# A gated trunk of three token mixers on one core: a score product on all 128 rows, and tiles laid at multiples of 128 bytes

## Chip, core and metric

The kernel runs on one core of a Trainium2 chip. The metric is the device time of one execution in microseconds; of several executions the median counts.

## What is computed

One layer over 1024 positions of 1024 channels, in float32. The input is normalised, one wide projection makes all operands, three branches mix the positions, each branch is gated and projected, and the merged sum goes through an output projection. The part that matters here is branch C, causal attention with 8 heads of 64 channels and a forgetting gate:

```python
h = rmsnorm(x, norm_g)
p = h @ w_in                       # gate_pre, a_in, a_z, b_uv, b_z, q, k, v, c_z, f_pre
q, k = rmsnorm(q, qn_g), rmsnorm(k, kn_g)          # per head of 64
c = cumsum(log_sigmoid(f_pre + b_f))               # per head
s = (q @ k.T) / 8 + c[query] - c[key]              # causal mask
o = softmax(s) @ v
y_c = (o * silu(c_z)) @ w_c
# y_a: GLU -> causal depthwise convolution (31 taps) -> layernorm -> silu, gated
# y_b: u * (tril(W_s) v + b) in chunks of 128 positions, gated
x = x + (g_a * y_a + g_b * y_b + g_c * y_c) @ w_out
```

## The kernel before

Float32 products are made of three products of a rounded type of the same four bytes: each operand is the sum of its rounding (hi) and the rest (lo), and hi x hi, hi x lo and lo x hi are added in one accumulator. So every weight tile comes as `raw` by DMA, is rounded by ScalarE (`w_hi`, L136), and GpSimd subtracts (`w_lo`, L137). `gemm_T` (L149) multiplies 128 output channels by 512 positions, with the normalised input `h_hi`, `h_lo` or a branch's operand as the moving tile.

The order of the stages is: the input's norm and transposes with the products for v (L267, L268); the projections of the first q and k; the gating unit's v and the mixing of positions (L404, L417); the attention; branch C's gate and projection together with branch A's GLU and its convolution on VectorE (31 taps, L646 and L649); branch B's second half; the norm of branch A; the merges; the output projection (L772). The instructions of all engines are put in order ahead of time by a planner with costs of its own, from the dependences between tiles and the priorities that the code gives. A tile that takes the place of an older one waits until the older one has no more readers. In the attention the heads have priority, and gates (`gate_pre`), the next heads' q and k and the gating unit's u (`u_slab`) are set between their products.

For a pair of heads, `stacks` builds 128-row operands. For head e of the pair its own 64 rows are `own`, the others `oth`. `ka` holds k hi on both halves; `qa` holds q hi on `own` and q lo on `oth`. So one product of 128 rows (L491) gives q hi x k hi + q lo x k hi. The third part, q hi x k lo, is a second product into the same accumulator with the 64 rows of `own` alone (L492), from a tile `kl` that the two heads of a pair share, each with its half. `head` goes through the query blocks from the last to the first, in up to two spans of keys; behind each span come the maximum (L494, VectorE), the exponential (L497, ScalarE), the scaling by the sum (L510, GpSimd), the transposes (L520), their rounding (L525, L526) and the product with v (L531).

The constants' pool comes first in the memory of a partition. Its square tiles have 512 bytes each, `eps` has 4, `vec` 168 and `cwT` 496; the pools for weights, h and what follows lie behind it, others are stacked from the other end of the memory. The moving tiles and the weights are multiples of 512 bytes, but for those of the products for v and the gating unit's v: `wv`, `wv_hi` and `wv_lo` have 520 columns, 2080 bytes.

Of the kernel before, what the change touches and what calls it, by code (L numbers as in the profile page):

```python
# [8 lines left out]
F32 = mybir.dt.float32  # L9
F32R = mybir.dt.float32r  # L10
# [5 lines left out]
P = 128  # L16
EPS = 1e-6
BIG = 3.0e38
NEG = -1.0e30
PRIO = 4000  # L20
# [7 lines left out]
def trunk_kernel(ctx, tc, x, norm_g, w_in, b_gate, conv_w, conv_b, conv_norm_g, conv_norm_b,  # L28
                 w_a, gmlp_norm_g, w_s, b_s, w_b, q_norm_g, k_norm_g, b_f, w_c, w_out, out):
    """float32 products are taken as three float32r passes: an operand is the exact sum of its  # L30
    rounding to 12 significant bits (hi) and the rest (lo), which has 12 bits as well, and
    hi*hi + hi*lo + lo*hi leaves out lo*lo alone, under float32's own rounding."""
# [28 lines left out]
    def f32(ap):  # L61
        return ap.bitcast(F32)

    # ---------------------------------------------------------------- pools
    # left: const, wpool, h, mix, then what a phase needs; right: v and o, later the merged sum
# [3 lines left out]

    const = ctx.enter_context(tc.tile_pool(name="const", bufs=1))  # L70
    wpool = ctx.enter_context(tc.tile_pool(name="wpool", bufs=3))
# [13 lines left out]
    # ---------------------------------------------------------------- constants  # L85
# [14 lines left out]
    eps = const.tile([P, 1], F32, name="eps")  # L100
    nc.vector.memset(eps, EPS)
    NVEC = 42
    vec = const.tile([P, NVEC], F32, name="vec")
    cwT = const.tile([P, JA, KW], F32, name="cwT")

    def newton(out_, ms, y0, y2, a, eng=None):
        """out_ = y0 brought nearer to (ms + EPS) ** -0.5."""
        if eng is None:
            nc.scalar.activation(y2, y0, AF.Square)
        else:  # L110
            eng.tensor_tensor(y2, y0, y0, op=ALU.mult)
        nc.vector.scalar_tensor_tensor(a, ms, EPS, y2, op0=ALU.add, op1=ALU.mult)
        nc.vector.tensor_scalar(a, a, -0.5, 1.5, op0=ALU.mult, op1=ALU.add)
        if out_ is not None:
            nc.vector.tensor_tensor(out_, y0, a, op=ALU.mult)

    def rsqrt(out_, ms, y0, y2, a):
        """out_ = (ms + EPS) ** -0.5: from the tables, then a Newton step."""
        nc.scalar.activation(y0, ms, AF.Ln, bias=eps)
        nc.scalar.activation(y0, y0, AF.Exp, scale=-0.5)  # L120
        newton(out_, ms, y0, y2, a)

    # ---------------------------------------------------------------- slabs of weights
    KH = 4

    def slab(src, kchunks, c0):
        """128 columns of a [kchunks * 128, n] matrix as hi and lo, K on partitions, KH chunks a tile."""
        out_ = []
        v = src.rearrange("(kc p) n -> p kc n", p=P)
        with tc.high_priority(offset=2 * PRIO):  # L130
            for k0 in range(0, kchunks, KH):
                raw = wpool.tile([P, KH, P], F32, name="raw")
                nc.sync.dma_start(out=raw, in_=v[:, k0:k0 + KH, c0:c0 + P])
                hi = wpool.tile([P, KH, P], F32R, name="w_hi")
                lo = wpool.tile([P, KH, P], F32R, name="w_lo")
                nc.scalar.copy(hi, raw)  # L136
                nc.gpsimd.tensor_tensor(lo, raw, f32(hi), op=ALU.subtract)  # L137
                out_.append((hi, lo))
        return out_

    def gemm_T(w, act, evac):
        """evac(half, psum, tokens): 128 output channels on partitions, 512 tokens."""
        for hf in range(NHALF):
            ps = mm.tile([P, HALF], F32, name="ps", tag="mm")
            ts = slice(hf * HALF, (hf + 1) * HALF)
            for kc in range(len(w) * KH):
                wk, k = w[kc // KH], kc % KH
                for n, (a, b) in enumerate(((0, 0), (0, 1), (1, 0))):
                    nc.tensor.matmul(ps, lhsT=wk[a][:, k, :], rhs=act[b][:, kc, ts],  # L149
                                     start=kc == 0 and n == 0, stop=kc == len(w) * KH - 1 and n == 2)  # L150
            evac(hf, ps, ts)

    # ---------------------------------------------------------------- q and k, normalised
# [25 lines left out]
    # ---------------------------------------------------------------- x -> h^T, v and f  # L179
    wnat = w2.rearrange("(kc p) n -> p kc n", p=P)  # L180
    cT_d = dram.tile([NH, S], F32, name="cT_d")
    # gates taken as far as their products between the attention's heads
    # (branch, chunk): the gates in the order in which they are wanted
# [3 lines left out]
    with ExitStack() as ph:  # L187
# [3 lines left out]
        NV = DC + NH  # L191
        N1 = DC // 2
        gb = p0.tile([P, D], F32, name="gb")
        bfb = p0.tile([P, NH], F32, name="bfb")
# [6 lines left out]
        class Weights:  # L201
            """hi and lo of columns c0.. of w_in (with those of f), a tile for every 128 rows, by way of mixT."""

            def __init__(self, c0, n, f0=None):
# [3 lines left out]
                last = p0x.tile([P, NV], F32, name="wv", bufs=1)  # L208
# [8 lines left out]
            def split(self, kc, eng):  # L217
                hi = p0x.tile([P, NV], F32R, name="wv_hi", bufs=KC)[:, 0:self.n]
                lo = p0x.tile([P, NV], F32R, name="wv_lo", bufs=KC)[:, 0:self.n]
                nc.scalar.copy(hi, self.raw[kc])  # L220
                eng.tensor_tensor(lo, self.raw[kc], f32(hi), op=ALU.subtract)
                self.hi.append(hi)
                self.lo.append(lo)
# [4 lines left out]
        def norm(i, r, pieces):  # L228
            """h of tile i in the place of x, in four steps"""
# [13 lines left out]
        def trans(i):  # L243
            """h^T of tile i, in two steps"""
# [10 lines left out]
        def prod(i, w, lag=0):  # L255
            """products of tile i with v and f, a step for every 128 rows of the weights, lo of them lag steps later"""
# [27 lines left out]
        with tc.high_priority(offset=8 * PRIO), tc.manual_schedule(engines=START):  # L284
            # norm, transposes and products of the tiles take turns, the first two of them in the order in which the
            # weights come in; the tensor engine's clock rises with work, which may as well be done before there is any
# [42 lines left out]
        # per-channel vectors, channel on partition  # L329
# [20 lines left out]
        # log sigmoid(z) = min(z, 0) - log1p(e), e = exp(-|z|);  # L350
        # log1p(e) = 2 atanh(s) = 2 s (1 + s^2/3 + s^4/5 + ...), s = e / (2 + e) <= 1/3
# [23 lines left out]
        # the scores stand at 8 times their value until the exponential  # L375
# [5 lines left out]
        # branch B's first half: v of the gating unit, its norm and the mixing of positions  # L381
        bsb = p0.tile([P, NG, P], F32, name="bsb")
        wsT = p0.tile([P, NG, 2, P], F32R, name="wsT")
# [44 lines left out]
    # ---------------------------------------------------------------- forgetting attention  # L428
    with ExitStack() as ph:
# [10 lines left out]
        for t in phis + plos:  # L440
            nc.gpsimd.memset(f32(t[:, 0, :]), 0.0)
        turn = [0, 0]

        def stacks(p, qn, kn):
            kl = stk.tile([P, S], F32R, name="kl", bufs=1)
            res = []
            for e in range(2):
                own = slice(e * HD, (e + 1) * HD)
                oth = slice((1 - e) * HD, (2 - e) * HD)
                ka = stk.tile([P, S], F32R, name="ka")  # L450
# [20 lines left out]
        def head(h, st, vc, oT):  # L471
# [3 lines left out]
            # from the last query block to the first: a block's own keys, once masked, are not asked for again  # L475
            for g in reversed(range(NT // 2)):
                pr = [None, None]
                for t in (2 * g + 1, 2 * g):
# [4 lines left out]
                    # a second span of 256 keys at least, which a float32r product's full rate asks for  # L483
# [3 lines left out]
                    for ci, (c0, n) in enumerate(spans):  # L487
# [4 lines left out]
                        nc.tensor.matmul(s[:, 0:w], lhsT=qa[own, qs], rhs=kl[own, cs], start=False, stop=True)  # L492
                        # the query's own cumulative gate is the same for all its keys, and goes with the maximum
# [7 lines left out]
                    else:  # L501
                        # two spans of keys, each by its own maximum, brought to the greater one
# [11 lines left out]
                for k2 in range(g + 1):  # L514
                    # the last pair of key blocks has nothing for the first query block in its second half
# [61 lines left out]
    # ---------------------------------------------------------------- branch C operand, branch A's input  # L577
# [3 lines left out]
    def gated(dst, src, w, tmp):  # L581
        """dst hi and lo = src * silu(h w); src takes the product."""
# [19 lines left out]
    # ---------------------------------------------------------------- merge  # L602
# [3 lines left out]
    def gate(bi, d, dst):  # L606
        """dst(half): where a half of the gate goes."""
# [22 lines left out]
    # ---------------------------------------------------------------- branch A: GLU and convolution; merge of C  # L630
# [30 lines left out]
    # ---------------------------------------------------------------- branch B: second half  # L661
# [7 lines left out]
    # ---------------------------------------------------------------- branch A: norm; merge of B  # L669
# [38 lines left out]
    # ---------------------------------------------------------------- branch A: gate and merge  # L708
# [47 lines left out]
    # ---------------------------------------------------------------- output projection  # L756
    ox_ctx, ox = pool("ox", bufs=3)
    for nh in range(D // HALF):
        ns = slice(nh * HALF, (nh + 1) * HALF)
        hi, lo = wos[nh]  # L760
        for i in range(NT):
# [3 lines left out]
            # the last tile in two pieces, for less to be left after the last product  # L765
# [46 lines left out]
```

## Time and profile before

| | |
|---|---|
| three runs | 1154.55, 1164.84, 1168.1 us, median 1164.84 |
| profiled execution | span 1162.8 us from the first to the last instruction; what lies around it isn't shown |
| mean granted TensorE clock | 0.984 |
| TensorE busy | 1116.7 us (96%), 5248 matmuls |
| VectorE, ScalarE, GpSimd busy | 606.8 us (52%), 462.0 us (40%), 501.5 us (43%) |
| products of 512 columns | L149: 3264, L404: 192, L772: 360 |
| score products | L491: 96, L492: 96 |

A span is counted from the first instruction to the last. Busy times overlap between engines, and matmuls overlap each other, so that a sum of their durations is more than the time they take.

### The profile page before, as it was taken

What the parts mean: (1) busy time and instruction counts of PE and PEld (TensorE: products, weight loads), DVE (VectorE), ACT (ScalarE), POOL (GpSimd) and SP (SyncE); (2) the same over time, 40 slices, a digit from 0 to 9 for tenths busy, and PEclk for the clock granted to TensorE, in tenths of its full rate; (3) what the DMA queues carried; (4) which work ended last, traced back from release to release, by engine and by line L of the source; (5) the groups of instructions that cost most, each with busy time, mean ns of one, the idle gap of its engine ahead of it and who ended that gap; (6) DMA issues with size and microseconds to landing.
All of it is one profiled execution on the core that took longest, in us unless ns stands there. A gap on an engine that the chain in (4) does not pass through costs nothing.

```text
span 1162.8 us, 14458 instructions
## 1 busy us (share of the span) xinstructions
PE 1116.7 (96%) x5248; PEld 902.8 (78%) x5248; DVE 606.8 (52%) x1079; ACT 462.0 (40%) x945; POOL 501.5 (43%) x447
## 2 busy tenths in 40 slices
PE   8999999999999999999999999999499798999998
PEld 7988887777777777777788788887387576877787
DVE  7665434644733364333331111799599995777211
ACT  5445345645743465444433123122023125875000
POOL 3032036546644564463331234332725499379100
PEclk9999999999999999999999999999799899999999
DMA  8210012121121212222213112132031143172222
GB/s 287 80 37 20 19 65 65 55 69 59 56 89 49 81 42 79 63 82 64 91 58 97 46 46 55 37 91 73 25 120 37 41 131 92 45 252 74 91 97 76
DMA packets 99506, 88.12 MB, mean 76 GB/s; under 512 B 6301, under 2 KB 76741, under 8 KB 99436
## 3 DMA queue, kind: packets, MB, share of 16 engines
q1 hardware_dynamic: 99436, 87.21, 24.3%
q8 instruction: 41, 0.67, 0.2%
q14 instruction: 29, 0.24, 0.1%
HBM read 70.38 MB, written 16.81 MB: 75 GB/s over the span
## 4 chain that ended last, share of the span: by engine, by line
PE 72%; DVE 14%; POOL 6%; DMA 3%; issue 2%; ACT 2%; SPq 1%; POOLq 0%; DVEq 0%; ACTq 0%
PE ps L149 44%; DVE acc L649 10%; PE ops L772 7%; PE tv L404 4%; PE o L531 4%; PE s L492 3%; PE tpp L520 3%; POOL w_lo L137 3%; PE pb L268 2%; PE pa L267 2%; PE s L491 2%; POOL part L626 1%; DMA gt<-gpre 1%; POOL part L747 1%; PE pm L417 1%
## 5 line engine op out<-in xcount | busy, mean ns | idle before, releaser
L149 PE MATMUL ps<-h_hi,w_lo 128*128 128x512 f32 x896 | 353.2, 395 | 19.3 <-POOL w_lo L137 19.3
L149 PE MATMUL ps<-h_hi,w_hi 128*128 128x512 f32 x896 | 353.4, 394 | 2.7 <-DVE part L623 1.3
L149 PE MATMUL ps<-h_lo,w_hi 128*128 128x512 f32 x896 | 353.7, 395 | 0.0
L137 POOL TENSOR_TENSOR w_lo<-raw,w_hi 128x512 fp32r<-128x512 f32 x136 | 216.8, 1597 | 264.8 <-ACT w_hi L136 260.4
L149 PEld LDWEIGHTS ps<-h_hi,w_lo 128*128 128x128 f32 x896 | 168.9, 189 | 57.6 <-POOL w_lo L137 20.2
L149 PEld LDWEIGHTS ps<-h_hi,w_hi 128*128 128x128 f32 x896 | 168.7, 188 | 39.8 <-issue 3.1
L149 PEld LDWEIGHTS ps<-h_lo,w_hi 128*128 128x128 f32 x896 | 168.8, 188 | 36.6 <-issue 2.7
L649 DVE SCALAR_TENSOR_TENSOR acc<-a_in,cwT,acc 128x1024 f32<-128x1024 f32 x120 | 183.4, 1570 | 0.6
L136 ACT CAST w_hi<-raw 128x512 fp32r<-128x512 f32 x136 | 83.5, 617 | 175.2 <-PE ps L149 111.6
L494 DVE CUSTOM_DVE_ANT_0 s<-s,cb 128x512 f32<-128x512 f32 (+2 forms) x96 | 54.0, 563 | 142.7 <-PE s L492 129.1
L510 POOL TENSOR_SCALAR pt<-pt,nm 128x512 f32<-128x512 f32 (+2 forms) x96 | 57.1, 604 | 78.9 <-DVE nm L508 51.7
L497 ACT ACTIVATE pt<-s,nm 128x512 f32<-128x512 f32 (+2 forms) x96 | 56.0, 585 | 49.4 <-DVE nm L494 36.7
L526 DVE TENSOR_TENSOR plo<-tpp,phi 128x512 fp32r<-128x512 f32 (+1 forms) x80 | 49.5, 633 | 41.5 <-ACT phi L525 41.2
L486 POOL TENSOR_TENSOR cb<-cb,mask 128x128 f32<-128x128 f32 x64 | 30.3, 474 | 73.6 <-DVE nm L494 55.2
L772 PE MATMUL ops<-wo_hi,mhi 128*128 128x512 f32 (+1 forms) x136 | 52.1, 383 | 1.7 <-ACT mhi L748 1.7
L772 PE MATMUL ops<-wo_hi,mlo 128*128 128x512 f32 (+1 forms) x136 | 52.1, 383 | 0.6 <-DVE mlo L749 0.6
L772 PE MATMUL ops<-wo_lo,mhi 128*128 128x512 f32 (+1 forms) x136 | 51.9, 381 | 0.0
L525 ACT CAST phi<-tpp 128x512 fp32r<-128x512 f32 (+1 forms) x80 | 41.8, 544 | 22.2 <-PE tpp L520 21.8
L149 PE MATMUL ps<-bb,w_hi 128*128 128x512 f32 x128 | 43.1, 421 | 6.7 <-ACT bb L587 6.6
L612 ACT ACTIVATE gt<-gt,vec 128x512 f32<-128x512 f32 x32 | 22.9, 723 | 67.0 <-DMA gt<-gpre 51.5
L774 DVE TENSOR_TENSOR xr<-ops,xr 128x512 f32<-128x512 f32 (+1 forms) x17 | 11.1, 659 | 67.7 <-PE ops L772 67.7
L531 PE MATMUL o<-phi,vc 128*128 128x256 f32 x160 | 44.4, 292 | 0.0
(212 smaller groups left out, 1861.1 us busy)
## 6 DMA issues: line engine op xcount, KB each, us to landing
raw<-in_w_in_dram SPq DMA_DIRECT2D x112, 256.0 KB, 2.8
gpre<-gst SPq DMA_DIRECT2D x48, 256.0 KB, 2.0
gt<-gpre SPq DMA_DIRECT2D x32, 256.0 KB, 2.9
xt<-in_x_dram SPq DMA_DIRECT2D x8, 512.0 KB, 3.5
cb<-cT_d SPq DMA_DIRECT2D x8, 512.0 KB, 4.7
xr<-in_x_dram SPq DMA_DIRECT2D x16, 256.0 KB, 2.7
wo_raw<-in_w_out_dram SPq DMA_DIRECT2D x16, 256.0 KB, 3.8
ga<-gpre SPq DMA_DIRECT2D x16, 256.0 KB, 6.2
```

What stands on the lines that cost most here:

```text
L136: nc.scalar.copy(hi, raw)
L137: nc.gpsimd.tensor_tensor(lo, raw, f32(hi), op=ALU.subtract)
L149: nc.tensor.matmul(ps, lhsT=wk[a][:, k, :], rhs=act[b][:, kc, ts], start=kc == 0 and n == 0, stop=kc == len(w) * KH - 1 and n == 2)
L404: nc.tensor.matmul(tv, lhsT=a[:, kc, ts], rhs=b[kc][:, 0:DB], start=kc == 0 and n == 0, stop=kc == KC - 1 and n == 2)
L494: nc.vector.tensor_tensor_reduce(out=s[:, 0:n], in0=s[:, 0:n], in1=cb[:, c0:c0 + n], scale=-float(HD) ** -0.5, scalar=BIG, op0=ALU.add, op ...
L497: nc.scalar.activation(pt[:, c0:c0 + n], s[:, 0:n], AF.Exp, bias=nm[:, ci:ci + 1], scale=-1.0, accum_out=nm[:, 2 + ci:3 + ci])
L510: nc.gpsimd.tensor_scalar(pt[:, c0:c0 + n], pt[:, c0:c0 + n], nm[:, 5 + ci:6 + ci], 1.0, op0=ALU.mult, op1=ALU.mult)
L525: nc.scalar.copy(phi[:, 1:n + 1], tp[:, 0:n])
L526: nc.vector.tensor_tensor(plo[:, 1:n + 1], tp[:, 0:n], f32(phi[:, 1:n + 1]), op=ALU.subtract)
L531: nc.tensor.matmul(o[:, 0:2 * P], lhsT=vc[:, kb, :], rhs=part[:, src, :], start=kb == 0 and z == 0, stop=kb == 2 * g + 1 and z == 1)
L649: nc.vector.scalar_tensor_tensor(acc[:, j], a_in[:, k:k + S], cwT[:, j, k:k + 1], acc[:, j], op0=ALU.mult, op1=ALU.add)
L772: nc.tensor.matmul(ps[:, 0:cols], lhsT=a[kc][:, ts], rhs=b[:, kc, cs], start=kc == 0 and n == 0, stop=kc == KC - 1 and n == 2)
```

## The change

There are two edits. First, the product q hi x k lo takes all 128 rows: `kl` is now two tiles that stay for the whole attention, one for each place in a pair, with zeros on the rows of the other head, written once by GpSimd; `stacks` writes the own half as before. Second, `eps` moves to a pool of 96 bytes at the other end of the memory, `vec`, `cwT`, `bfb`, `wv`, `wv_hi` and `wv_lo` are laid out wider so that each row is a multiple of 128 bytes, and `wsT` takes the place of `gb`. Comments and docstrings are gone too, and line numbers move by a few.

```diff
+LINE = 128
...
     const = ctx.enter_context(tc.tile_pool(name="const", bufs=1))
+    edge = ctx.enter_context(tc.tile_pool(name="edge", bufs=1, side="right"))
...
-    eps = const.tile([P, 1], F32, name="eps")
+    eps = edge.tile([P, 24], F32, name="eps")[:, 0:1]
...
-    vec = const.tile([P, NVEC], F32, name="vec")
-    cwT = const.tile([P, JA, KW], F32, name="cwT")
+    vec = const.tile([P, 2 * LINE // 4], F32, name="vec")[:, 0:NVEC]
+    cwT = const.tile([P, JA, LINE // 4], F32, name="cwT")[:, :, 0:KW]
...
+        NVP = DC + LINE // 4
...
-        gb = p0.tile([P, D], F32, name="gb")
-        bfb = p0.tile([P, NH], F32, name="bfb")
+        gb = p0.tile([P, D], F32, name="gb", tag="gbw")
+        bfb = p0.tile([P, LINE // 4], F32, name="bfb")[:, 0:NH]
...
-                last = p0x.tile([P, NV], F32, name="wv", bufs=1)
+                last = p0x.tile([P, NVP], F32, name="wv", bufs=1)
...
-                hi = p0x.tile([P, NV], F32R, name="wv_hi", bufs=KC)[:, 0:self.n]
-                lo = p0x.tile([P, NV], F32R, name="wv_lo", bufs=KC)[:, 0:self.n]
+                hi = p0x.tile([P, NVP], F32R, name="wv_hi", bufs=KC)[:, 0:self.n]
+                lo = p0x.tile([P, NVP], F32R, name="wv_lo", bufs=KC)[:, 0:self.n]
...
-        wsT = p0.tile([P, NG, 2, P], F32R, name="wsT")
+        wsT = p0.tile([P, NG, 2, P], F32R, name="wsT", tag="gbw")
...
+        kls = [g1.tile([P, S], F32R, name=f"kl{e}") for e in range(2)]
+        for e, t in enumerate(kls):
+            nc.gpsimd.memset(f32(t[(1 - e) * HD:(2 - e) * HD]), 0.0)
         turn = [0, 0]
 
         def stacks(p, qn, kn):
-            kl = stk.tile([P, S], F32R, name="kl", bufs=1)
             res = []
             for e in range(2):
                 own = slice(e * HD, (e + 1) * HD)
                 oth = slice((1 - e) * HD, (2 - e) * HD)
+                kl = kls[e]
...
-                        nc.tensor.matmul(s[:, 0:w], lhsT=qa[own, qs], rhs=kl[own, cs], start=False, stop=True)
+                        nc.tensor.matmul(s[:, 0:w], lhsT=qa[:, qs], rhs=kl[:, cs], start=False, stop=True)
```

## Rows read from the trace of the kernel before

**Rows 1.** Busy time by stage: stretch, then each engine's busy us (instructions), granted clock.

```profile
160.00:620.00 460.00, 460.00 (x2195) 361.76 (x2194) 199.91 (x560) 234.29 (x532) 229.69 (x272) 1.00 0.22 68
733.00:930.00 197.00, 169.23 (x719) 137.57 (x718) 180.19 (x142) 41.02 (x69) 83.17 (x39) 0.93 0.21 62
...
1078.00:1162.80 84.80, 81.50 (x373) 66.65 (x372) 12.55 (x19) 0.62 (x1) 1.97 (x2) 1.00 0.27 90
```

**Rows 2.** Pieces of the chain that ended last: start us, us, engine, tile, line, count.

```profile
132.27 5.58 PE tv L404 x24
...
625.10 41.55 PE ps L149 x183
...
1078.87 80.80 PE ops L772 x370
```

**Rows 3.** Line L492: durations min/median/max ns, first and last start, forms.

```profile
L492 PE MATMUL s<-kl,qa x96: 379/440/501, 177.4 to 610.5; 64*128 64x512 f32 x40, 64*128 64x256 f32 x32, 64*128 64x384 f32 x24
```

**Rows 4.** Timeline of TensorE around two L492 products: start us, duration us.

```profile
243.16 0.28 PE L531 MATMUL o<-plo,vc 128*128 128x256 f32 x1
243.28 0.40 PE L491 MATMUL s<-ka,qa 128*128 128x512 f32 x1
243.61 0.49 PE L492 MATMUL s<-kl,qa 64*128 64x512 f32 x1
244.03 0.50 PE L149 MATMUL ps<-h_lo,w_hi 128*128 128x512 f32 x1
244.37 0.39 PE L149 MATMUL ps<-h_hi,w_lo 128*128 128x512 f32 x1
...
248.44 0.28 PE L491 MATMUL s<-ka,qa 128*128 128x256 f32 x1
248.65 0.38 PE L492 MATMUL s<-kl,qa 64*128 64x256 f32 x1
248.96 0.50 PE L149 MATMUL ps<-h_hi,w_lo 128*128 128x512 f32 x1
249.30 0.39 PE L149 MATMUL ps<-h_hi,w_hi 128*128 128x512 f32 x1
```

**Rows 5.** Waits of TensorE's weight loads, 160 to 620 us: total us, times, longest.

```profile
PEld s L492 <- issue: 20.8, 81, 0.4
...
PEld s L492 <- POOL kl L460: 0.6, 2, 0.4
```

**Rows 6.** Timelines of GpSimd and TensorE: a scaling and the transposes behind it.

```profile
246.71 1.26 POOL L510 TENSOR_SCALAR pt<-pt,nm 128x512 f32<-128x512 f32 x2 [0.20 <-DVE nm L508]
...
252.12 1.04 PE L520 MATMUL tpp<-ident,pt 128*128 128x128 f32 x8
```

**Rows 7.** GpSimd's fills: line L367, and the timeline at the attention's start.

```profile
L367 POOL MEMSET zer<- x1: 941/941/941, 40.4 to 40.4; 8x1024 f32 x1
...
163.90 0.35 POOL L441 MEMSET phi<- 128x128 f32 x2 [6.58 <-PE pm L417]
```

**Rows 8.** Lines L240 (reads gb) and L393 (writes wsT): first and last start.

```profile
L240 DVE SCALAR_TENSOR_TENSOR xt<-xt,r,gb x18: 477/744/1748, 7.0 to 58.0; 128x512 f32<-128x512 f32 x14, 128x256 f32<-128x256 f32 x4
...
L393 ACT CAST wsT<-tw x1: 588/588/588, 93.2 to 93.2; 128x512 fp32r<-128x512 f32 x1
```

**Rows 9.** Timeline: a product of 128 rows and the weight load of the next.

```profile
299.84 0.39 PE L149 MATMUL ps<-h_lo,w_hi 128*128 128x512 f32 x1
299.84 0.19 PEld L149 LDWEIGHTS ps<-h_hi,w_lo 128*128 128x128 f32 x1
```

**Rows 10.** Chain: a subtraction of GpSimd; timeline: VectorE's taps; stretches as in rows 1.

```profile
813.56 18.29 POOL w_lo L137
...
810.31 20.41 DVE L649 SCALAR_TENSOR_TENSOR acc<-a_in,cwT,acc 128x1024 f32<-128x1024 f32 x17
...
813.50:831.90 18.40, 1.01 (x5) 0.49 (x4) 17.22 (x15) 0.99 (x2) 18.34 (x2) 0.66 0.00 0
831.90:836.60 4.70, 4.70 (x11) 3.74 (x12) 0.00 (x0) 0.00 (x0) 1.17 (x1) 0.50 0.38 112
```

## Prediction

> **What bounds the kernel now.** I read the table by stage first. Between 160 and 620 us, the attention, TensorE is busy 460.00 of 460 us at a granted clock of 1.00 (the 2.4 GHz level), while VectorE, ScalarE and GpSimd stand at 200 to 234 us each [rows 1]. What TensorE stops doing there comes off the end, as long as nothing else fills the gap. From 733 to 930, the convolution, TensorE has gaps (169 of 197 us) and VectorE is at 180 of 197; in the last 85 us TensorE is the bound again [rows 1].
>
> Second, the chain that ended last, for the time from one matmul to the next. A busy time of a matmul won't do for that: matmuls overlap, so I divide pieces of the chain by their counts. 183 products of 512 columns take 41.55 us, 0.227 us each; 24 of the gating unit 5.58 us, 0.2325 each; the output projection's 370 take 80.80 us, of which 48 have 256 columns (the last tile comes in two pieces, 2 x 24), so at 0.12 us for those the other 322 take 0.233 each [rows 2, 4].
>
> Third, the line that the change edits, L492: 96 products, 40 of 512, 24 of 384 and 32 of 256 columns, all on 64 rows [rows 3]. The timeline shows what they cost, if starts are subtracted. For 512 columns: L491 starts at 243.28, L492 0.33 later, the next product 0.42 after that, the one behind it 0.34 later. Each would take 0.227 in a plain run. So the 64-row product makes the product ahead of it 0.10 us longer, itself 0.19 and the product behind it 0.11 [rows 4]. With 256 columns the starts are 0.21, 0.31 and 0.34 apart where 0.12 (an L531 product of 256 columns, from 243.16 to 243.28), 0.12 and 0.227 are usual: 0.09, 0.19, 0.11 [rows 4]. The surplus doesn't grow with the columns, so it is a price for going from 128 rows to 64 and back, not for streaming. A second view agrees: the weight loads of L492 stood idle 81 times, 20.8 us, with no releaser that the profile knows ("issue") [rows 5].
>
> **The change part by part.** *The scores' second product on 128 rows.* It has the columns that it had, and all its neighbours have 128 rows, so the surplus goes: 40 x 0.41 + 24 x 0.40 + 32 x 0.39 = 38.5 us. The 384-column value is taken between the other two. All of it lies on TensorE in the stage where it never rests.
>
> Is there something that waits next? For TensorE no wait is listed in that stage at all. The longest chain behind a score goes over the maximum, the exponential and GpSimd's scaling to the transposes. In one turn the scaling ends at 246.71 + 1.26 = 247.97 and the transposes that read it start at 252.12: 4.15 us to spare [rows 6]. Two 64-row products lie between, whose 0.8 us goes, and 3.3 us is left. So nothing is late next, and the 38.5 us counts whole.
>
> *Two kl tiles that stay, with zeros on the other head's rows.* Added: two GpSimd fills of 64 x 1024. The nearest row is the 8 x 1024 fill at 0.941 us, so 1.9 us for both; they stand at the fills of phi and plo, ahead of which GpSimd idles 6.58 us [rows 7]. Queued behind them are one weight subtraction, the first q subtractions (L457) and kl's (L460), and then the first head's scores; TensorE works on gates meanwhile. So 0 to 1.9 us, and I take 0.5, near the covered end, since kl kept the loader waiting for only 0.6 us in the whole stage [rows 5]. The subtractions into kl keep their number and size. They no longer wait for the other head's last product, but GpSimd is at half load there: 0.
>
> *Places.* wsT takes gb's slot. gb is last read by the norm that starts at 58.0, wsT is first written at 93.2 [rows 8], so the new wait is over 34 us before it matters: 0. eps, bfb, vec, cwT and the wider strides change no count and no size of an instruction.
>
> *Starts at multiples of 128 bytes.* In the kernel before, weights and h share one remainder that is not zero, because eps, vec and cwT ahead of them have odd sizes. Their products run at 0.227 us. The gating unit's moving tiles are 2080 bytes apart and so start at four different remainders, the multiple of 128 among them, and run at 0.2325 on average, no better [rows 2]. In no row is a 512-column product faster than 0.227, wherever its operands start. Bounds: the time that 256 more columns take is 0.227 - 0.12 = 0.107, so 512 columns without any fixed part would take 0.214; on some 3,800 products of that width (the table ahead) a gain of at most 13 ns each is 49 us. The other way, some 3,260 products of L149 might go from 0.227 to the 0.233 of the projection: 20 us lost. In the projection weights and moving tiles come from the two ends of the memory and are shifted against each other; the 0.006 us on 322 products there is 1.9 us that may be had. I take 1 us of gain, near the row in which four remainders gain nothing.
>
> Sum against the profiled execution's span: 1162.8 - 38.5 + 0.5 - 1 = 1123.8 us. The median of the runs shown lies 2.0 above that span, and I carry it along: **1126 us**.
>
> **The rivals.** *The rows are not the cause (1165).* If the surplus belonged to something else of this product, such as its operands, nothing would move. Against it: L491 has the same shape of result and the same queries, and the piece of 0.227 each is full of 128-row products into one accumulator. Chance 0.05.
>
> *The full load is not covered.* A 128-row weight load takes 0.19 us and in the trace starts with the product before its own, under it, at 0.23 us a product [rows 9]. If the load that now takes all rows had to wait for the product in flight, 96 x 0.19 = 18 us would come back: 1144. The Trainium skill, TensorE: Matmul & The Clock Gate, The mechanism, says that a load overlaps matmuls in flight only where its row group differs, which speaks against this change; by that rule the result would be this 1144. The 128-row loads in [rows 9] don't follow it. Chance 0.04.
>
> *The attention is no longer bound by TensorE.* If half of the gap filled with waits for the exponential's chain, 19 us would come back: 1145. The 3.3 us to spare speak against it; the order of instructions, planned ahead of time for other tiles, may differ and speaks for it. Chance 0.06.
>
> *GpSimd is held off in the convolution.* One weight subtraction (w_lo) started at 813.56 and lasted 18.29 us, while VectorE ran 17 taps without a break from 810.31 to 830.7 [rows 10]. TensorE did 5 products in 18.4 us, and after it 11 products took 4.70 us at granted 0.50 (the 1.2 GHz level) where they'd take 2.5 [rows 10]. The price of such a hold is about 17.4 + 2.2 = 19.6 us. The Trainium skill, SBUF — State Buffer, SBUF: two separate sides, describes an exclusive lock between VectorE and GpSimd that is held for one instruction; here the wait outlasts a dozen, and the measurement decides. Whether it happens hangs on which engine starts first, and the change shifts this stage by some 38 us and may alter its order. Without the hold 1106 (0.13); with one more 1146 (0.08). This is also the mechanism for the slower side: it decides from the third hold more, 1126 + 3 x 19.6 = 1185, since two only cancel the gain. For it speaks that 733 to 930 holds long stretches of taps; against it, that the stage's own work and relative times are untouched. Chance 0.04.
>
> *The starts matter after all.* By the bounds above: down by up to 49 us, 1078, or up by 20 us, 1146. Chances 0.04 and 0.03.
>
> **How the numbers follow.** The forecast has the rest, 0.53, with a range of its own of 1116 to 1136: the runs shown spread from 1154.6 to 1168.1, -10 to +3 about their median, and the bounds of the fills and of the projection add 2. The range that should hold the time 8 times in 10 takes in the case without the hold and those at 1144 to 1146: **1103 to 1147**. Left out are 1078, 1165 and 1185, together 0.13, and the outer edges of the others. A change of 1% is 11.6 us, about what a measurement of this kernel can tell from no change. Below 1153 are all cases but 1165 and 1185: faster 0.91, same 0.05, slower 0.04.
>
> **What would show it.** In the profile after, L492 appears on 128 rows; 512-column scores start 0.23 us after L491 and the next product 0.23 after them; the "issue" idle of its loads is gone; the attention's last score comes some 38 us earlier while TensorE stays without waits. Pieces of the chain with L149 stay at 0.227 (a fall below 0.22 would prove me wrong on the starts), and the projection's 322 are between 0.227 and 0.233. It is wrong if new waits for POOL pt or ACT phi show on TensorE, or if the number of w_lo subtractions beyond 10 us changes.

## The result and the profile after

| | before | after |
|---|---|---|
| runs | 1154.55, 1164.84, 1165.23, 1168.1 | 1115.31, 1116.94, 1127.19, 1127.24 us |
| median | 1165.03 (four runs) | 1122.07 us |
| ratio | | 0.9639, 95% interval 0.9578 to 0.9700 |
| span of the profiled execution | 1162.8 | 1113.6 us (own time 1115.31) |
| mean granted TensorE clock | 0.984 | 0.989 |
| TensorE busy | 1116.7 us, 96% | 1076.0 us, 97% |

The change makes the kernel 43 us faster, 3.6%. Both kernels' runs fall into two groups some 11 us apart: about 1154 and 1165 before, 1116 and 1127 after. Two of the four runs after lie in each, so that their median, 1122, lies in the gap, where no run is. The profile of before is of the upper group, that of after of the lower one, so that some 11 us of the 49 between the two profiles have nothing to do with the change. Group by group the difference is 38.0 us (1127.2 against 1165.2) and 38.4 (1116.1 against 1154.55).

Line numbers moved: L404 is L409, L491 and L492 are L500 and L501, L149 is L153, L137 is L141, L649 is L658, L772 is L781. The product of the change, in the view of one line: durations min/median/max in ns, first and last start in us, forms. In [rows 3] all its forms have 64 rows and the median was 440.

```profile
L501 PE MATMUL s<-kl,qa x96: 279/338/476, 177.1 to 570.2; 128*128 128x512 f32 x40, 128*128 128x256 f32 x32, 128*128 128x384 f32 x24
```

The stages, to be read against [rows 1] (busy us of PE, weight loads, VectorE, ScalarE, GpSimd, then the granted clock):

```profile
160.00:580.00 420.00, 418.45 (x2174) 356.75 (x2173) 198.67 (x560) 231.82 (x530) 228.79 (x274) 1.00 0.24 73
698.00:885.00 187.00, 171.25 (x725) 137.94 (x724) 185.42 (x144) 41.16 (x68) 71.40 (x40) 0.96 0.23 69
1030.00:1113.60 83.60, 79.99 (x373) 66.76 (x373) 12.83 (x19) 0.88 (x2) 2.53 (x2) 1.00 0.27 92
```

TensorE is still the engine that bounds the attention, but it now rests a little: it is busy 418.45 of 420 us, where it was 460.00 of 460. The timeline of TensorE shows both the 1.5 us that are missing (in brackets) and what was won (the last four lines):

```profile
179.63 0.39 PE L153 MATMUL ps<-h_hi,w_hi 128*128 128x512 f32 x1
179.86 0.39 PE L153 MATMUL ps<-h_lo,w_hi 128*128 128x512 f32 x1
180.09 0.39 PE L500 MATMUL s<-ka,qa 128*128 128x512 f32 x1
180.31 0.40 PE L501 MATMUL s<-kl,qa 128*128 128x512 f32 x1
181.49 0.50 PE L153 MATMUL ps<-h_hi,w_hi 128*128 128x512 f32 x1 [0.78 <-DVE gst L556]
181.83 0.39 PE L153 MATMUL ps<-h_lo,w_hi 128*128 128x512 f32 x1
182.06 0.34 PE L500 MATMUL s<-ka,qa 128*128 128x384 f32 x1
182.23 0.34 PE L501 MATMUL s<-kl,qa 128*128 128x384 f32 x1
183.34 0.50 PE L153 MATMUL ps<-h_hi,w_lo 128*128 128x512 f32 x1 [0.77 <-POOL w_lo L141]
183.67 0.39 PE L153 MATMUL ps<-h_hi,w_hi 128*128 128x512 f32 x1
...
188.02 0.39 PE L500 MATMUL s<-ka,qa 128*128 128x512 f32 x1
188.25 0.40 PE L501 MATMUL s<-kl,qa 128*128 128x512 f32 x1
188.48 0.39 PE L153 MATMUL ps<-h_lo,w_hi 128*128 128x512 f32 x1
188.71 0.62 PE L153 MATMUL ps<-h_hi,w_lo 128*128 128x512 f32 x2
```

From 188.02 on the starts of L500, L501 and the two products behind them are 0.23 us apart, where they were 0.33, 0.42 and 0.34 [rows 4]. The two bracketed waits are new: one for VectorE's gst, one for GpSimd's w_lo. There the starts are 1.18 and 1.11 us apart where 0.23 and 0.17 are usual; the two waits cost 1.9 us, and the product behind each is 0.11 longer. The list of waits of TensorE's weight loads from 160 to 585 us (total, times, longest) now has these two lines alone. The 20.8 us of "issue" of [rows 5] are gone:

```profile
PEld ps L153 <- DVE gst L556: 1.2, 1, 1.2
PEld ps L153 <- POOL w_lo L141: 1.1, 1, 1.1
```

Pieces of the chain that ended last (start, us, count), against [rows 2]:

```profile
131.91 5.56 PE tv L409 x24
...
584.45 46.53 PE ps L153 x205
...
1031.44 79.04 PE ops L781 x370
```

46.53 / 205 is 0.227 us a product, as before. The gating unit's 24 take 0.232 each, as before, though its tiles now start at other places. In the projection (79.04 - 5.76) / 322 is 0.2276 where it was 0.233. The last score starts 40.3 us earlier than before, at 570.2 in place of 610.5 [rows 3]. That is more than the rows won, since 22 more products of 0.227 us now stand behind it (205 in place of 183).

Where the 49.2 us between the spans lie can be read from four marks:

| mark (start, but for the last) | before | after | difference since the mark above |
|---|---|---|---|
| first convolution product on VectorE | 733.94 | 698.28 | -35.7 |
| last tap | 959.66 | 911.37 | -12.6 |
| first projection product | 1066.81 | 1018.84 | +0.3 |
| end of the span | 1162.79 | 1113.60 | -1.2 |

The -12.6 are the difference between the groups: the subtraction of 18.29 us in [rows 10] isn't in the profile after, where none is longer than 2.4.

### The profile page after: what moved, and what is told of

Its sections match the earlier page's. It is cut to its first block, busy times and chain, and to the rows that moved or that the text cites. A ratio compares the mean times of both kernels' runs of the same rounds, so it can differ in the third digit from the quotient of the medians.

```text
span 1113.6 us, 14467 instructions
## 1 busy us (share of the span) xinstructions
PE 1076.0 (97%) x5248; PEld 900.1 (81%) x5248; DVE 607.8 (55%) x1079; ACT 460.7 (41%) x945; POOL 487.1 (44%) x449
## 4 chain that ended last, share of the span: by engine, by line
PE 71%; DVE 17%; POOL 4%; issue 3%; ACT 2%; DMA 2%; SPq 0%; POOLq 0%; ACTq 0%; DVEq 0%
PE ps L153 45%; DVE acc L658 12%; PE ops L781 7%; PE tv L409 4%; PE o L540 3%; PE tpp L529 3%; PE pa L272 2%; PE pb L273 2%; PE s L501 2%; PE s L500 2%; POOL part L635 1%; DMA gt<-gpre 1%; POOL part L756 1%; PE pm L422 1%; POOL w_lo L141 1%
## 5 line engine op out<-in xcount | busy, mean ns | idle before, releaser
L153 PE MATMUL ps<-h_hi,w_hi 128*128 128x512 f32 x896 | 351.7, 392 | 5.2 <-ACT w_hi L140 2.2
L153 PE MATMUL ps<-h_hi,w_lo 128*128 128x512 f32 x896 | 351.8, 393 | 4.5 <-POOL w_lo L141 4.5
L153 PE MATMUL ps<-h_lo,w_hi 128*128 128x512 f32 x896 | 351.5, 392 | 0.0
L141 POOL TENSOR_TENSOR w_lo<-raw,w_hi 128x512 fp32r<-128x512 f32 x136 | 202.7, 1492 | 253.1 <-ACT w_hi L140 251.7
L153 PEld LDWEIGHTS ps<-h_hi,w_hi 128*128 128x128 f32 x896 | 168.6, 188 | 40.7 <-ACT w_hi L140 4.3
L153 PEld LDWEIGHTS ps<-h_hi,w_lo 128*128 128x128 f32 x896 | 168.8, 188 | 39.1 <-POOL w_lo L141 6.1
L153 PEld LDWEIGHTS ps<-h_lo,w_hi 128*128 128x128 f32 x896 | 168.8, 188 | 33.6
L658 DVE SCALAR_TENSOR_TENSOR acc<-a_in,cwT,acc 128x1024 f32<-128x1024 f32 x120 | 187.2, 1600 | 0.6
L506 ACT ACTIVATE pt<-s,nm 128x512 f32<-128x512 f32 (+2 forms) x96 | 56.0, 585 | 54.1 <-DVE nm L503 38.5
L781 PE MATMUL ops<-wo_hi,mhi 128*128 128x512 f32 (+1 forms) x136 | 51.5, 379 | 2.4 <-ACT mhi L757 2.4
L781 PE MATMUL ops<-wo_hi,mlo 128*128 128x512 f32 (+1 forms) x136 | 51.5, 378 | 0.6 <-DVE mlo L758 0.6
L781 PE MATMUL ops<-wo_lo,mhi 128*128 128x512 f32 (+1 forms) x136 | 51.3, 377 | 0.0
L153 PE MATMUL ps<-bb,w_hi 128*128 128x512 f32 x128 | 42.5, 417 | 7.5 <-ACT bb L596 6.7
L153 PE MATMUL ps<-ab,w_hi 128*128 128x512 f32 x128 | 40.9, 404 | 2.5 <-ACT w_hi L140 2.5
```

Source lines behind the costliest of these rows:

```text
L506: nc.scalar.activation(pt[:, c0:c0 + n], s[:, 0:n], AF.Exp, bias=nm[:, ci:ci + 1], scale=-1.0, accum_out=nm[:, 2 + ci:3 + ci])
L658: nc.vector.scalar_tensor_tensor(acc[:, j], a_in[:, k:k + S], cwT[:, j, k:k + 1], acc[:, j], op0=ALU.mult, op1=ALU.add)
L781: nc.tensor.matmul(ps[:, 0:cols], lhsT=a[kc][:, ts], rhs=b[:, kc, cs], start=kc == 0 and n == 0, stop=kc == KC - 1 and n == 2)
```

## The experiments

**One part at a time.** The first kernel is the one before with the row edit alone.

```diff
+        kls = [g1.tile([P, S], F32R, name=f"kl{e}") for e in range(2)]
+        for e, t in enumerate(kls):
+            nc.gpsimd.memset(f32(t[(1 - e) * HD:(2 - e) * HD]), 0.0)
...
-            kl = stk.tile([P, S], F32R, name="kl", bufs=1)
...
+                kl = kls[e]
...
-                        nc.tensor.matmul(s[:, 0:w], lhsT=qa[own, qs], rhs=kl[own, cs], start=False, stop=True)
+                        nc.tensor.matmul(s[:, 0:w], lhsT=qa[:, qs], rhs=kl[:, cs], start=False, stop=True)
```

> The kernel before with the 128-row product and the two kl tiles alone; the places of all other tiles as before. If the 64 rows are the price (0.40 us for each of 96 products), it is 36 to 39 us faster than the kernel before, some 1127, and in its profile the score products of 512 columns stand 0.23 us apart while the output projection stays at 0.233 us a product. If the starts at multiples of 128 bytes carried a part of the gain, it lacks that part: half of it would be some 1146. Products of L149 on h stay at 0.227.

Measured: 1129.8 us (1129.5 to 1131.0, four runs, all of the upper group), ratio 0.973 (0.9667 to 0.9794). That is 35 below the upper group of before, a little less than the 36 to 39 that were expected.

The second has the changed kernel's places, but the 64-row product and the shared `kl` of before.

```diff
-                        nc.tensor.matmul(s[:, 0:w], lhsT=qa[:, qs], rhs=kl[:, cs], start=False, stop=True)
+                        nc.tensor.matmul(s[:, 0:w], lhsT=qa[own, qs], rhs=kl[own, cs], start=False, stop=True)
```

> The changed kernel's places, with the 64-row product and the shared kl tile of the kernel before. If the starts are worth only what the projection shows, it is 1 to 3 us faster than the kernel before (1162 to 1165) and its projection goes from 0.233 to 0.227 us a product; score products keep the surplus of 0.40 us. If the starts matter everywhere, L149 on h falls below 0.22 us and it is some 40 us faster (1125).

Measured: 1162.7 us (1150.7 to 1163.2, ten runs), ratio 0.9992 (0.9948 to 1.0035). Group by group it is about 2.3 faster than before, 1162.7 against 1165.0 and 1152.1 against 1154.3; over all runs that isn't told from no change.

The third is the changed kernel with that same line alone put back; the two filled tiles stay.

> The changed kernel with one line put back: the second score product reads the 64 rows of its own head, from the two kl tiles that stay. If the rows are the price, it is 36 to 40 us slower than the changed kernel, within 4 us of the kernel before, with the idle weight loads (issue, some 20 us) back. If the tiles that stay (no wait for the shared kl) brought the gain, it stays near 1122.

Measured: 1163.4 us (1152.3 to 1164.1, ten runs), ratio 0.998 (0.9943 to 1.0016). Beside the changed kernel's 1127.2 and 1116.1, the one line is worth 36.2 us in the upper group and 36.4 in the lower. The view of the line, and two lines of the list of the loads' waits from 160 to 620 us, show the old price back:

```profile
L501 PE MATMUL s<-kl,qa x96: 379/438/502, 177.3 to 606.0; 64*128 64x512 f32 x40, 64*128 64x256 f32 x32, 64*128 64x384 f32 x24
```

```profile
PEld s L501 <- issue: 22.1, 85, 0.4
PEld ps L153 <- issue: 7.7, 35, 0.2
```

All of the gain beyond some 2 us is the rows. The rival by which something else of this product costs the time has fallen, and so has that of the uncovered load.

**Is the price one per change of rows, or one per product of 64 rows?** In the kernel before, each 64-row product is cut into two of half the columns, on the same rows.

```diff
-                        nc.tensor.matmul(s[:, 0:w], lhsT=qa[own, qs], rhs=kl[own, cs], start=False, stop=True)
+                        for z in range(2):
+                            zs = slice(z * w // 2, (z + 1) * w // 2)
+                            nc.tensor.matmul(s[:, zs], lhsT=qa[own, qs],
+                                             rhs=kl[own, c0 + z * w // 2:c0 + (z + 1) * w // 2],
+                                             start=False, stop=z == 1)
```

> The kernel before with each 64-row product cut into two of half the columns, one behind the other: 192 products of 64 rows, in 112 unbroken groups where there were 96. If the price belongs to the change between 128 and 64 rows, it is 112 x 0.40 = 45 us in place of 38.5, and some 0.01 us for each product more: 7 to 9 us slower than the kernel before (1172 to 1174). If each 64-row product has the price, 192 x 0.40 = 77 us: 38 us slower (1203).

Measured: 1173.5 us (1162.7 to 1177.2, ten runs), ratio 1.0073 (1.0038 to 1.0109): 8.5 us more, not 38. TensorE's timeline shows why (x2 is the pair of halves):

```profile
243.91 0.49 PE L491 MATMUL s<-ka,qa 128*128 128x512 f32 x1
244.33 0.50 PE L494 MATMUL s<-kl,qa 64*128 64x256 f32 x2
244.76 0.50 PE L149 MATMUL ps<-h_lo,w_hi 128*128 128x512 f32 x1
245.09 0.39 PE L149 MATMUL ps<-h_hi,w_lo 128*128 128x512 f32 x1
```

From the first half to the next product of 128 rows it is 0.43 us; the whole product took 0.42 [rows 4]. A second 64-row product behind a first costs little more than its columns, 0.01 us here. In the trace the 192 halves stand in 112 unbroken groups instead of 96; 16 more at the prediction's 0.40 are 6.4 of the 8.5 us. So the price belongs to the change from 128 rows to 64 and back. The Trainium skill, TensorEngine Tiling (Array Packing), Key Properties, says that changing the tiling mode drains TensorE and gives no figure. The 0.40 us per group of 64-row products between 128-row ones would fit that; what the engine does in this time no trace here shows.

**Which starts are it?** The projection went from 0.233 to 0.2276 us a product in the changed kernel and in the one with the places alone, but not in the one with the rows alone. The prediction named multiples of 128 bytes. What the weights and the moving tiles of the changed kernel's projection also share is the remainder of 256. The starts are added up from the widths of the tiles in the code; no view of the profile shows them. In the next kernel the far end of the memory is moved by 128 bytes more: all starts stay multiples of 128, but the projection's weights and moving tiles differ by 128 in the remainder of 256.

```diff
-    eps = edge.tile([P, 24], F32, name="eps")[:, 0:1]
+    eps = edge.tile([P, 56], F32, name="eps")[:, 0:1]
```

> The changed kernel with eps's tile at 224 bytes in place of 96: everything stacked from the far end moves by 128 bytes and still starts at a multiple of 128. If it is the multiple of 128 that brought the projection from 0.233 to 0.227 us a product, it stays at 0.227 and the time within 1 us of the changed kernel's. If it is how the weights' starts and the moving tiles' starts lie to each other (equal remainders of 256), the projection and the products on bb and ab go back to 0.233 and the kernel is some 2 us slower than the changed one.

The other way round, the kernel before gets a pad of 128 bytes at the far end: starts that are no multiples of 128, with equal remainders of 256.

```diff
+    edge = ctx.enter_context(tc.tile_pool(name="edge", bufs=1, side="right"))
+    pad = edge.tile([P, 32], F32, name="pad")
+    nc.vector.memset(pad, 0.0)
```

> The kernel before with a tile of 128 bytes of its own at the far end and one small fill more, nothing else: all large tiles keep starts that are 96 past a multiple of 128, but both ends now have the same remainder of 256. If multiples of 128 matter, the projection stays at 0.233 us a product. If the starts matter to each other, it goes to 0.227, and the kernel is some 2 us faster than the kernel before (1162.5 beside 1165).

And in the changed kernel the far end is moved by 64 bytes, with 40 in the place of 24 in the same line.

> The changed kernel with the tiles of the far end moved by 64 bytes more, so that their starts stand 64 past multiples of 128 and the remainders of 256 of the weights' and the moving tiles' starts differ by 64 in the last projection. If any difference of the remainders of 256 costs (theory): the projection's 512-column products follow each other at 0.232 to 0.234 us in the mean, as where they differ by 128. If it is only the difference of 128 that costs (rival): 0.227 to 0.228 us. If starts off multiples of 128 cost by themselves (second rival): above 0.234 us.

The projection's piece of the chain, in this order (the kernel with 128 more, the kernel before with the pad, the one with 64 more), 322 products of 512 columns in each:

```profile
1043.77 80.81 PE ops L781 x370
```

```profile
1078.54 79.05 PE ops L775 x370
```

```profile
1044.42 79.64 PE ops L781 x370
```

That is 0.233, 0.2276 and 0.2294 us each. Multiples of 128 with unequal remainders of 256 are slow, other starts with equal remainders fast. A difference of 64 lies between; each of the three accounts named for it gave another figure, so how the price grows with the difference stays open.

The projection isn't the only place. Branch B's and branch A's last products (on `bb` and `ab`) also have moving tiles at the far end and weights at the near one. Here are the starts of the first and the 46th of an unbroken row of products on `ab`: before, after, and with 64 more.

```profile
1017.42 0.62 PE L149 MATMUL ps<-ab,w_hi 128*128 128x512 f32 x2
1027.91 0.63 PE L149 MATMUL ps<-ab,w_lo 128*128 128x512 f32 x2
```

```profile
970.31 0.61 PE L153 MATMUL ps<-ab,w_hi 128*128 128x512 f32 x2
980.54 0.62 PE L153 MATMUL ps<-ab,w_lo 128*128 128x512 f32 x2
```

```profile
982.54 0.63 PE L153 MATMUL ps<-ab,w_hi 128*128 128x512 f32 x2
993.04 0.63 PE L153 MATMUL ps<-ab,w_lo 128*128 128x512 f32 x2
```

45 steps take 10.49, 10.23 and 10.50 us, 0.233, 0.227 and 0.233 each. On `ab` a difference of 64 bytes thus costs as much as one of 128. Nor does the remainder explain every product: the rows of the changed `wv_hi` and `wv_lo` have 2176 bytes, 128 more than a multiple of 256, so that every second moving tile of the gating unit has the remainder of its weights, and still the 24 take 0.232 each. In whole time the three kernels took 1129.5 us with 128 more (1119.2 to 1131.3, six runs; ratio 0.9701, 0.9653 to 0.9749), 2.3 above the changed kernel's upper group; 1162.5 with the pad (1150.6 to 1164.2, twelve runs; ratio 0.9972, 0.9935 to 1.0010), 2.5 below that of before; 1128.9 with 64 more (one run).

**What makes the two groups?** Each of the nine profiles of an execution of the upper group has one subtraction of some 18 us in the convolution, the one profile of the lower group none. To take this hold away, the changed kernel's subtractions for the GLU and for branch C's merge go to VectorE.

```diff
-    def slab(src, kchunks, c0):
+    def slab(src, kchunks, c0, eng=None):
...
-                nc.gpsimd.tensor_tensor(lo, raw, f32(hi), op=ALU.subtract)
+                (eng or nc.gpsimd).tensor_tensor(lo, raw, f32(hi), op=ALU.subtract)
...
-        gemm_T(slab(wm[0], br[0].shape[1], d * P), br, evac)
+        gemm_T(slab(wm[0], br[0].shape[1], d * P, nc.vector if first else None), br, evac)
...
-            w = slab(w2, KC, A0 + DA + j * P)
+            w = slab(w2, KC, A0 + DA + j * P, nc.vector)
...
-            w = slab(w2, KC, A0 + j * P)
+            w = slab(w2, KC, A0 + j * P, nc.vector)
```

> The changed kernel with the w_lo subtractions of the GLU and of branch C's merge (24 of them from the convolution's stage) on VectorE in place of GpSimd. The single runs so far fall into two groups some 11 us apart. If GpSimd's subtraction that is held off behind an unbroken run of taps makes the slower group, no subtraction beyond 3 us is left, all runs lie within some 3 us, and VectorE's taps lose part of their time above 1.28 us each. VectorE takes 24 x 0.69 = 17 us more work, the taps give back up to 30: 1105 to 1120. If the groups have another cause, two groups stay.

Measured: 1119.2 us (1117.8 to 1120.3, six runs), ratio 0.9623 (0.9583 to 0.9664). There is one group only, some 3 us above the lower one of the changed kernel, and in its profile no subtraction longer than 3 us. So the hold makes the two groups. That the 3 us are the price of VectorE's added work in its busiest stage is likely, but not shown by itself.

**The two new waits.** The first pair's `kl` subtraction goes to VectorE, to shorten GpSimd's queue at the attention's start.

```diff
-                    nc.gpsimd.tensor_tensor(kl[own, ts], kn[own, ts], f32(ka[own, ts]), op=ALU.subtract)
+                    (nc.gpsimd if p else nc.vector).tensor_tensor(kl[own, ts], kn[own, ts], f32(ka[own, ts]), op=ALU.subtract)
```

> The changed kernel with the first pair's kl subtractions on VectorE, which has nothing to do at the attention's start. If the two new waits of TensorE behind the first scores (0.9 us each) come from GpSimd's full queue there, they go and the kernel is 1 to 3 us faster than the changed one in runs of the same group. If they come from the order alone, they stay and the time with them.

Measured: 1126.4 us (1113.2, then 1125.6 to 1126.9; six runs), ratio 0.9667 (0.9616 to 0.9718). The two waits are gone and the convolution starts at 696.30 instead of 698.28. The median is above the changed kernel's because five of the six runs lie in the upper group; group by group it is 0.8 to 3 better (one run in the lower group).

This kernel's profile has the hold, the changed kernel's hasn't, at the same place. VectorE's taps, then GpSimd's subtractions, in the timeline of the kernel with the hold:

```profile
772.66 20.41 DVE L658 SCALAR_TENSOR_TENSOR acc<-a_in,cwT,acc 128x1024 f32<-128x1024 f32 x17
...
775.62 19.81 POOL L141 TENSOR_TENSOR w_lo<-raw,w_hi 128x512 fp32r<-128x512 f32 x2 [5.31 <-ACT w_hi L140]
```

and in that of the changed kernel:

```profile
774.82 25.56 DVE L658 SCALAR_TENSOR_TENSOR acc<-a_in,cwT,acc 128x1024 f32<-128x1024 f32 x17
...
778.41 4.62 POOL L141 TENSOR_TENSOR w_lo<-raw,w_hi 128x512 fp32r<-128x512 f32 x2 [5.33 <-ACT w_hi L140]
786.46 2.39 POOL L141 TENSOR_TENSOR w_lo<-raw,w_hi 128x512 fp32r<-128x512 f32 x1 [3.43 <-ACT w_hi L140]
789.18 1.90 POOL L141 TENSOR_TENSOR w_lo<-raw,w_hi 128x512 fp32r<-128x512 f32 x1 [0.33 <-ACT w_hi L140]
794.62 2.28 POOL L141 TENSOR_TENSOR w_lo<-raw,w_hi 128x512 fp32r<-128x512 f32 x1 [3.54 <-ACT w_hi L140]
```

The same 17 taps meet the same subtraction. Either GpSimd gets in, here five times in the run, and the taps that it meets take 2.3 us instead of 1.27, so that the run is 5.15 us longer; or the subtraction stands until the run of taps ends, and all taps take 1.27. Both happen within one execution: in the profile of before, the subtractions from 777.78 on get in, and the one at 813.55 is held. The Trainium skill, SBUF — State Buffer, SBUF: two separate sides, describes an exclusive lock between the two engines for the length of one instruction. The 1.0 us that a tap is late for a subtraction of 1.3 agrees with it. A subtraction that outlasts more than a dozen taps does not. What decides between the two isn't shown. In the nine profiles with the hold the subtraction starts 3.0 to 3.4 us behind the first of the 17 taps, in the one without it 3.6.

**Both together.** To the kernel above is added that the subtractions of the late GLU slabs (j of 2 and 3) go to VectorE, and of all of the convolution's stage only these.

```diff
-            w = slab(w2, KC, A0 + DA + j * P)
+            w = slab(w2, KC, A0 + DA + j * P, nc.vector if j >= 2 else None)
...
-            w = slab(w2, KC, A0 + j * P)
+            w = slab(w2, KC, A0 + j * P, nc.vector if j >= 2 else None)
```

> The first pair's kl subtraction on VectorE, as in e8, and of the subtractions that cut w_lo from a GLU slab those of j >= 2 on VectorE too (j of 0 and 1, branch C's and all others stay on GpSimd). If the held subtraction of GpSimd is one of these late GLU slabs and nothing else (theory): no subtraction of GpSimd longer than 3 us, one group of runs instead of two, in the lower group's place, 1111 to 1117 us, and so faster than the changed kernel (1122) by some 5 to 11 us and than the version with all w_lo of the convolution on VectorE (1119.2) by 2 to 8. If the hold falls to whichever subtraction meets the run of taps (rival): another subtraction, branch C's or that of j = 1, is held for some 18 us in most runs, two groups remain, and the median stands at 1122 to 1127. If VectorE's added instructions in the taps' stage cost as much as they did with all of w_lo there (second rival): one group, 1117 to 1120.

Measured: 1115.0 us (1114.7 to 1115.8, five runs), ratio 0.9582 (0.9555 to 0.9610), 7 us below the changed kernel's median. One group; the line's view (min/median/max in ns) has no long subtraction, on either engine:

```profile
L141 POOL TENSOR_TENSOR w_lo<-raw,w_hi x128: 1261/1296/2283, 21.8 to 1015.4; 128x512 fp32r<-128x512 f32 x128
...
L141 DVE TENSOR_TENSOR w_lo<-raw,w_hi x8: 674/679/683, 721.0 to 771.8; 128x512 fp32r<-128x512 f32 x8
```

Eight subtractions at 0.68 us on VectorE were enough, and neither branch C's nor those of j = 0 and 1 were held in their place. It is 4.2 us below the kernel with all 24 on VectorE, but not for that alone: that one still has the two waits of 1.9 us.

## Why the prediction was right

**The rows.** The step gave 38.5 us, 0.40 for each of 96 products, counted whole. Undoing the one line costs 36.2 to 36.4 us, and the timeline after shows that each product now takes its columns' time. The difference is in the next step: "nothing is late next" was wrong by 1.9 us, the two waits behind the products at 180.31 and 182.23, and 0.2 behind them. The kernel with the line undone has one of them too, at 0.4 us. With the 1.5 that the waits cost beyond that, and the 0.2, the runs give about 38. The prediction looked for waits on the far side of the scores, at the exponential, the scaling and the transposes. There none came, but the margin was thinner than the 3.3 us that it left. In the turn of [rows 6] it is 243.62 - (240.96 + 1.25), 1.4 us, since the planner now sets fewer other products between:

```profile
240.96 1.25 POOL L519 TENSOR_SCALAR pt<-pt,nm 128x512 f32<-128x512 f32 x2
...
243.62 1.04 PE L529 MATMUL tpp<-ident,pt 128*128 128x128 f32 x8
```

The waits came on the near side, at the start of the stage, where GpSimd's queue feeds the first heads.

**The fills.** Taken at 0.5 us with a bound of 1.9; they took 1.19 each, 2.4, and GpSimd's queue at the attention's start ran 0.35 later. That cover was thinner than the step said: it is in this queue that one of the two waits ends. With the fills and 64 rows, the kernel with the one line undone, TensorE waits there for w_lo too, but 0.4 us instead of 0.8, and not for gst; so the fills are part of it and the rest comes with the faster products. In whole time 0.5 was about right: the two kernels with 64 rows and the new places, one with the tiles that stay and one without, are 0.7 us apart in the upper group (1163.4 and 1162.7) and 0.5 in the lower (1152.6 and 1152.1).

**The starts.** Taken at 1 us of gain, measured 2.3 to 2.5. The step named multiples of 128 bytes as the thing that might matter and the projection as the only place where it could. The projection was a right place: 322 x 0.0054 is 1.7 us. It wasn't the only one. The step counted all of L149 at 0.227, but 384 of its products, those on `bb` and `ab`, stood at 0.233 as well and went to 0.227. How much of the other 0.6 us is theirs isn't shown: TensorE isn't the bound in all of their stage. The thing that mattered was not the one named: equal remainders of 256 bring the projection to 0.2276, multiples of 128 alone don't. L153 on h stayed at 0.227, and the bounds of -49 and +20 were far off.

**The convolution's hold.** "Without the hold" was priced at 19.6 us below the forecast. The groups stand 10.7 to 13 apart, and the convolution's stage is 12.6 shorter in the profile without it. The step counted what TensorE lost, but in this stage VectorE is the bound, and it worked on while GpSimd was held. VectorE's own loss stands in its timeline of before, behind the run of taps:

```profile
844.71 0.69 DVE L623 TENSOR_TENSOR part<-ps,gt 128x512 f32<-128x512 f32 x1 [13.98 <-PE ps L149]
```

In the profile after it has no such wait. Against the 14.0 us stands that its taps take longer there (before and after; busy us, mean ns), since no subtraction is held off them:

```profile
L649 DVE SCALAR_TENSOR_TENSOR acc<-a_in,cwT,acc 128x1024 f32<-128x1024 f32 x120 | 183.4, 1570 | 0.6
...
L658 DVE SCALAR_TENSOR_TENSOR acc<-a_in,cwT,acc 128x1024 f32<-128x1024 f32 x120 | 187.2, 1600 | 0.6
```

14.0 - 3.8 is 10.2 of the 12.6; where the other 2.4 lie isn't shown. The step also took the hold for a property of the kernel, with one chance for all its runs. It is one of each execution: 1154.55 among the runs shown was a run of the lower group. The forecast's own case, the hold kept, says 1126, and that group measured 1127.2.

**Luck.** That the median, 1122, fell 4 us below the forecast hangs on two of four runs being without the hold; three would have brought it to about 1116. And 1126 beside 1127.2 owes something to errors that cancel. The rows with the fills gave 35.5 to 36.0 us (the changed kernel beside the one with its places alone, group by group) where the sum has 38.0; the starts gave 1.3 more than it has.

**The rivals.** The load of all rows stays covered by the product in flight: L500 and L501 load 128 rows each and start 0.22 to 0.23 us apart. The rule of the Trainium skill in TensorE: Matmul & The Clock Gate, The mechanism, by which a load overlaps only where its row group differs, is not borne out; the same section also names a load into a background weight buffer, and nothing here speaks against that. The attention stayed bound by TensorE but for 1.5 us in 420. No third or fourth hold came. The starts did not decide.

## What to carry to other kernels

In a stage where TensorE never rests, a product on half the rows between products on all rows costs more than the full one: 0.63 us of time for 512 columns instead of 0.23. Zeros on the unused rows are cheaper than the change of rows, if the fill is done once. Look then at the queues that feed the stage's first products: the faster products come sooner to what these still have to make. Where the runs of a kernel fall into two groups, look for one long instruction in the profile of one group that the other lacks, and move it, or the few that can take its place, to another engine.

## What was not expected of the hardware

- A 64-row product between 128-row ones costs 0.40 us beyond its columns, with 256 columns as with 512; a second 64-row product right behind it cost 0.01 more than its columns in the row shown.
- In the output projection a product of 512 columns follows the last at 0.2276 us where weights and moving tile start at the same remainder of 256 bytes, and at 0.233 where these differ by 128, whether or not the starts are multiples of 128. The gating unit's products, 0.232 us in every layout, don't follow this.
- A GpSimd subtraction of 1.3 us either delays a tap of VectorE from 1.27 to 2.3 us, or is itself held for 18 us until the run of taps ends. Which of the two a given subtraction meets differs between executions of one program, as the two groups of runs show, and within one.
